# Attention scores of two heads issued alternately on the two halves of TensorE's rows, in a four-layer fp32 decoder trunk

## The chip, the cores and the metric

One core of one Trainium2 chip. The metric is the device time of one execution in microseconds (us), lower is better; times of several runs are given as their median. TensorE (PE) multiplies, VectorE (DVE), ScalarE (ACT) and GpSimd (POOL) work on tiles, SyncE (SP) issues the transfers.

## The reference

Four layers on 256 tokens of width 1024. Each layer has a token mixer with 16 heads of 64 and then a dense SwiGLU feed-forward; after each of the two, `x = LN(alpha * x + f(x))`. The mixers are, in order: sliding-window attention with four key/value heads and a sink logit per head (A), a mixture of three dilated windows merged by their softmax denominators (B), block-sparse attention that at this length is plain causal attention (C), and A again.

```python
    s = jnp.einsum('bnqhgd,bnkhd->bnhgqk', qb, kb) * (dh ** -0.5)
...
    s = jnp.where(ok[None, :, None, None], s, NEG)
    m = s.max(-1)
    if sink is not None:
...
        m = jnp.maximum(m, sk)
    p = jnp.exp(s - m[..., None])
    l = p.sum(-1)
    if sink is not None:
        l = l + jnp.exp(sk - m)
    o = jnp.einsum('bnhgqk,bnkhd->bnqhgd', p, vb) / jnp.transpose(l, (0, 1, 4, 2, 3))[..., None]
```

This is the attention that all three mixers use, over blocks of queries and keys. The dot product of a score runs over the 64 numbers of one head.

## The kernel before, in words

Every fp32 operand of a matrix product is held as two fp16 parts, high and low. A product is three fp16 matmuls into one PSUM bank: high by high, high by low, low by high (`mm3`, lines 127 to 132). Weights come in chunks of 128 x 4096; ACT and DVE make the two parts (`load_w`, lines 91 and 92).

A layer is a projection of the tokens into queries, keys and values (`proj`), attention (`attend`), the output projection (`out_steps`), a layer norm, and the feed-forward (`ffn`). Attention never runs alone: `weave` issues the steps of `attend` evenly between steps of other products. In the mixers' middle part these are the projections of the next heads; at the end (`finish`) they are the output projection. One such fill step is three matmuls of 128 x 512. PE, DVE, ACT and POOL each take their instructions strictly from a list; which instruction stands where in the list is decided when the program is built, from the order in which the steps are issued and from what each waits for, so that pieces of several steps can stand mixed.

Queries and keys lie transposed: tile `qkh` (high part) and `qkl` (low part) hold four pairs of heads, 128 rows by 256 tokens each; rows 0 to 63 are the pair's first head, rows 64 to 127 its second. `halves` picks one head's 64 rows.

`attend` works on items (lines 212 to 305). In A and C an item is two heads of one query tile t of 128 tokens, in B one head with its three groups. Each item goes through four steps, and between them lie whole items: `scores` at once, `flip` two items later (LF), `values` three (LV), `collect` four (LO).

- `scores`: for each head, and each group, one `mm3` of 64 rows into a PSUM bank of 512 columns (pool `ats`, four banks, tile name `at`). With t = 0 it is 128 columns wide, with t = 1 256. DVE then scales, masks and takes the running minimum of the negated scores (line 252), ACT makes the exponentials and their sum (line 255). For A, POOL copies the sinks of the item's two heads beside the scores (line 235).
- `flip`: PE transposes the exponentials in blocks of 128 x 128, up to four blocks in one `at` bank (line 268); ACT and DVE split the bank into parts `ph` and `pl` (lines 135 and 137).
- `values`: `mm3` of `ph`, `pl` with the values into `pv`, 64 columns each; after four heads DVE normalises (line 289).
- `collect`: two transposes of the four heads' result and the split into `oth`, `otl`, the output projection's operand (line 299).

`mixer_a` and `mixer_bc` build the items; the tiles `s` of the scores have four buffers.

Of the kernel before, what the change touches and what calls it, by code (L numbers as in the profile page):

```python
# [18 lines left out]
P = 128  # L19
# [13 lines left out]
# Weights are scaled by a power of two before they are split into two fp16  # L33
# parts, so that the low part stays in fp16's normal range.
# [9 lines left out]
def trunk(ctx, tc, a, out):  # L44
# [99 lines left out]
    def weave(main, fill):  # L144
        """issue two lists of steps, evenly interleaved"""
        nf = 0
        for i, step in enumerate(main):
            step()
            while nf < len(fill) and nf * len(main) < (i + 1) * len(fill):
                fill[nf]()  # L150
                nf += 1
        for step in fill[nf:]:
            step()

    def transpose_x(t, XT, half):
        """columns of X[t] (512 of them) -> XT, in two parts"""
# [32 lines left out]
    def rope(y, t, nh):  # L189
        """y [128, nh, 64] fp32, in place"""  # L190
# [11 lines left out]
    def transpose_qk(y, t, dst):  # L202
        """y [128 tokens, 4 pairs of heads x 128] -> dst parts [128, 4, 256 tokens]"""
# [8 lines left out]
    def attend(items, oT):  # L212
        """steps for softmax attention. items: (query tile, heads, keys of their transposes), with heads [(head, groups, sinks)]
        and groups [(qT, kT, v)]: qT, kT parts [64, 256], v parts [128, NT, 64]; sinks [128, heads]
        (negated) or None. The groups' keys share one softmax. Four heads in a row, of one query tile,
        make a quad, whose outputs are normalised and transposed together."""
        st, quads = {}, {}

        def quad(i):
            t, heads = items[i][:2]  # L220
            return quads.setdefault((t, heads[0][0] // 4), {})

        def scores(i):
            t, heads = items[i][:2]
            flush([(k, tt) for k in items[i][2] for tt in range(t + 1)])
            nk, ng, nh = (t + 1) * P, len(heads[0][1]), len(heads)
            per, n = 512 // nk, nk * ng
            sk, mk = heads[0][2], MASK[heads[0][3]][t]
            q = quad(i)
            if "l" not in q:  # L230
                q["l"] = sm.tile([P, 4], F32, name="l", bufs=6)
            s = sm.tile([P, 768], F32, name="s", bufs=4)
            s = s[:, :nh * (n + (sk is not None))].rearrange("p (h n) -> p h n", h=nh)
            if sk is not None:
                nc.gpsimd.tensor_copy(s[:, :, n], sk)
            mn = sm.tile([P, 4], F32, name="mn", bufs=6)
            ps = None
            for hi, (h, groups, _, _) in enumerate(heads):
                m = None
                for g, (qT, kT, _) in enumerate(groups):  # L240
                    u = hi * ng + g
                    if u % per == 0:
                        ps = ats.tile([P, 512], F32, name="at")
                    o = u % per * nk
                    mm3(ps[:, o:o + nk], sl2(qT, ALL, tok(t)), sl2(kT, ALL, slice(0, nk)), True, True)
                    if u % per == per - 1 or g == ng - 1:
                        # the groups of this head in this bank
                        g0 = max(0, g - u % per)
                        c0, c1 = g0 * nk, (g + 1) * nk
                        init = (3e38 if sk is None else sk[:, hi:hi + 1]) if m is None else m  # L250
                        m = mn[:, 2 * hi + (g0 > 0):2 * hi + (g0 > 0) + 1]
                        nc.vector.tensor_tensor_reduce(  # L252
                            s[:, hi, c0:c1], ps[:, o + nk - (c1 - c0):o + nk], mk[:, c0:c1], scale=-QSC,
                            scalar=init, op0=OP.add, op1=OP.min, accum_out=m)
                nc.scalar.activation(s[:, hi], s[:, hi], AF.Exp, bias=m, scale=-1.0,  # L255
                                     accum_out=q["l"][:, h % 4:h % 4 + 1])
            st[i] = s

        def flip(i):
            t, heads = items[i][:2]  # L260
            nq = len(heads[0][1]) * (t + 1)
            nb = len(heads) * nq
            s, parts = st[i], []
            for b0 in range(0, nb, 4):
                bn = min(4, nb - b0)
                ps = ats.tile([P, 4, P], F32, name="at")
                for b in range(bn):
                    nc.tensor.transpose(ps[:, b], s[:, (b0 + b) // nq, tok((b0 + b) % nq)], ident)
# [3 lines left out]
                parts += [(ph[:, b], pl[:, b]) for b in range(bn)]  # L272
            st[i] = parts

        def values(i):
            t, heads = items[i][:2]
            q, parts = quad(i), st.pop(i)
            if "o" not in q:
                q["o"] = pv[:, turn[0]]
                turn[0] = 1 - turn[0]  # L280
            for h, groups, _, _ in heads:
                nb = len(groups) * (t + 1)
                for b in range(nb):
                    g, kt = divmod(b, t + 1)
                    mm3(q["o"][:, h % 4], parts.pop(0), sl2(groups[g][2], ALL, kt), b == 0, b == nb - 1)
            if h % 4 == 3:
                nc.vector.reciprocal(q["l"], q["l"])
                q["y"] = sm.tile([P, 4, DH], F32, name="oy", bufs=2)
                nc.vector.tensor_tensor(q["y"], q["o"], q["l"].unsqueeze(2).to_broadcast([P, 4, DH]), op=OP.mult)

        def collect(i):
            t, heads = items[i][:2]
            h, q = heads[-1][0], quad(i)
            if h % 4 != 3:
                return
            ps = ats.tile([P, 2, P], F32, name="at")
            y = q["y"].rearrange("p h d -> p (h d)")
            for j in range(2):
                nc.tensor.transpose(ps[:, j], y[:, tok(j)], ident)  # L299
            pr = slice(h // 4 * 2, h // 4 * 2 + 2)  # L300
            split(oT[0][:, pr, tok(t)], oT[1][:, pr, tok(t)], ps)
# [8 lines left out]
    def halves(tq, pr, hh):  # L310
        return sl2(tq, slice(hh * DH, (hh + 1) * DH), pr)
# [3 lines left out]
    def layer_norm(idx, folded=False):  # L315
        """(begin, one(t)): X[t] <- LN(alpha * X[t] + PS[.., t]), and its transposed parts"""
# [38 lines left out]
    def out_steps(PS, lhs, nk, w, h, t, ks, k0=0):  # L355
        """steps of PS[h, t] += lhs.T @ w over the k-tiles ks (of w's, w starting at k0)"""
# [67 lines left out]
    def finish(li, oT, items, kA, folded=False):  # L424
        """the last heads' attention, beside the output projection of the others, and LN"""
# [16 lines left out]
    def mixer_a(li, j, XT):  # L442
# [28 lines left out]
        def items(c):  # L471
            out = []
            for t in range(NT):
                for pr in range(4):
                    heads = []
                    for hh in range(2):
                        h = 8 * c + 2 * pr + hh
                        g = h // 4
                        heads.append((h, [(halves(qTs[c], pr, hh), halves(kT, g, hh), sl2(vv, ALL, ALL, g))],
                                      nsink[:, h - hh:h - hh + 2], 0))  # L480
                    out.append((t, heads, (c, 2)))
# [23 lines left out]
    def mixer_bc(li, XT, ng):  # L505
        """MoBA with one block per sequence has no past block to choose (its selection is masked
        for every query by the shapes alone), which leaves causal attention within the block;
        the dilated groups' softmax merge is one softmax over the groups' keys."""
# [48 lines left out]
        def items(quad):  # L557
            out = []
            for t in range(NT):
                for pr in range(2):  # L560
                    heads = []
                    for hh in range(2):
                        gl = []
                        for g in range(ng):
                            v, off = vs[g, quad]
                            qk = qks[g, quad]
# [153 lines left out]
```

## Time and profile before

| | |
|---|---|
| time, median of 3 runs | 1289.83 us (1288.73 to 1291.22) |
| span of the profiled execution | 1288.2 us (no other time of it is given; the median lies 1.6 us above) |
| PE busy | 1265.8 us, 98% of the span |
| DVE, ACT, POOL busy | 873.0, 664.0 and 112.7 us: 68%, 52%, 9% |
| matmuls | 10352, of them 576 of 64 rows (the scores) |
| granted TensorE clock, mean | 0.997 of full speed |
| DMA | 233 MB, 181 GB/s mean |

A row of the timeline says when an instruction, or several alike, began and how long they took to the last one's end; matmuls are pipelined, so what one costs is read from the start of one to the start of the next. A row of groups has the number of instructions, their busy time and the mean of one, and behind the bar the idle time of the engine just before them and what ended it. A row of stretches has the busy time of each engine in that stretch.

### The profile page before, as it was taken

To read this page: it belongs to the slowest core of one execution; us is meant where nothing else is said; L and a number is where in the kernel's file an instruction comes from. 1 tells how busy PE (TensorE), PEld (TensorE's weight loads), DVE (VectorE), ACT (ScalarE), POOL (GpSimd) and SP (SyncE) were. 2 spreads that over 40 slices of the span, in tenths; PEclk is the share of its full clock that TensorE was granted. 3 is DMA by queue.
4 is the path that set the end of the run, shared out by engine and by line. 5 is a ranking of instruction groups with operands and counts; after the bars stand their busy time and mean duration, and the time that the engine had idled before them with its cause. 6 is when DMAs were issued, how large, how long until landed. Compare 5 with 4: busy or idle time off the path is not lost. (4 is left out here: it accounts for less than half of the span.)

```text
span 1288.2 us, 24678 instructions
## 1 busy us (share of the span) xinstructions
PE 1265.8 (98%) x10352; PEld 844.9 (66%) x10352; DVE 873.0 (68%) x1451; ACT 664.0 (52%) x1117; POOL 112.7 (9%) x230
## 2 busy tenths in 40 slices
PE   7989999999999999999999999999999999999997
PEld 3549988444555555589884445589884445898843
DVE  5888766475565666777665667777665687876652
ACT  5765654345555565446544456536544366464430
POOL 1410000012011101000000020100000041000000
PEclk9999999999999999999999999999999999999999
DMA  8445755656345334347555564247555552475520
GB/s 316 166 164 197 263 200 184 221 206 222 145 147 173 139 131 151 112 163 251 209 181 180 201 225 162 100 164 257 203 180 182 223 207 99 153 250 207 190 87 33
DMA packets 35663, 233.31 MB, mean 181 GB/s; under 512 B 4448, under 2 KB 4448, under 8 KB 9696
## 3 DMA queue, kind: packets, MB, share of 16 engines
q1 hardware_dynamic: 35552, 231.74, 51.0%
q8 instruction: 81, 1.33, 0.4%
q14 instruction: 30, 0.25, 0.1%
HBM read 230.68 MB, written 1.05 MB: 180 GB/s over the span
## 5 line engine op out<-in xcount | busy, mean ns | idle before, releaser
L92 DVE SCALAR_TENSOR_TENSOR wlo<-raw,whi 128x1024 f16<-128x1024 f32 x416 | 500.3, 1223 | 206.1 <-ACT whi L91 205.8
L91 ACT ACTIVATE whi<-raw 128x1024 f16<-128x1024 f32 x416 | 414.6, 1049 | 258.9 <-PE acc L132 92.1
L131 PE MATMUL acc<-xtl,whi 128*128 128x256 f16 (+1 forms) x1792 | 408.2, 250 | 0.0
L132 PE MATMUL acc<-xth,wlo 128*128 128x256 f16 (+1 forms) x1792 | 408.2, 250 | 0.0
L130 PE MATMUL acc<-xth,whi 128*128 128x256 f16 (+1 forms) x1792 | 408.0, 250 | 0.1
L130 PE MATMUL acc<-whi,xth 128*128 128x512 f16 x480 | 183.3, 382 | 2.4 <-ACT xth L135 2.4
L131 PEld LDWEIGHTS <-whi 128*128 128x128 f16 x1792 | 175.3, 98 | 12.5 <-issue 0.3
L130 PEld LDWEIGHTS <-whi 128*128 128x128 f16 x1792 | 175.3, 98 | 11.9
L131 PE MATMUL acc<-wlo,xth 128*128 128x512 f16 x480 | 183.0, 381 | 0.2 <-DVE wlo L92 0.2
L132 PE MATMUL acc<-whi,xtl 128*128 128x512 f16 x480 | 182.8, 381 | 0.3
L132 PEld LDWEIGHTS <-wlo 128*128 128x128 f16 x1792 | 175.3, 98 | 11.6
L130 PE MATMUL acc<-whi,hth 128*128 128x512 f16 x352 | 133.4, 379 | 0.0
L131 PE MATMUL acc<-wlo,hth 128*128 128x512 f16 x352 | 133.4, 379 | 0.0
L132 PE MATMUL acc<-whi,htl 128*128 128x512 f16 x352 | 133.4, 379 | 0.0
L255 ACT ACTIVATE s<-s,mn 128x257 f32<-128x257 f32 (+5 forms) x128 | 67.6, 529 | 46.3 <-DVE mn L252 46.1
L333 POOL TENSOR_TENSOR mv<-mv,nhalf 128x1 f32<-128x1 f32 x16 | 15.8, 986 | 817.5 <-DVE mv L332 817.5
L132 PEld LDWEIGHTS <-xtl 128*128 128x128 f16 x480 | 47.3, 99 | 57.8 <-DVE xtl L137 3.0
L130 PEld LDWEIGHTS <-xth 128*128 128x128 f16 x480 | 47.2, 98 | 48.4 <-issue 5.0
L135 ACT ACTIVATE hth<-hf 128x256 f16<-128x256 f32 x88 | 36.5, 415 | 74.5 <-DVE hf L377 74.5
L131 PEld LDWEIGHTS <-xth 128*128 128x128 f16 x480 | 47.2, 98 | 40.3 <-issue 1.5
L137 DVE TENSOR_TENSOR pl<-at,ph 128x512 f16<-128x512 f32 (+2 forms) x96 | 51.5, 551 | 19.0 <-ACT ph L135 18.5
L132 PEld LDWEIGHTS <-htl 128*128 128x128 f16 x352 | 34.4, 98 | 41.5
(93 smaller groups left out, 1499.0 us busy)
## 6 DMA issues: line engine op xcount, KB each, us to landing
raw<-in_w_gu SPq DMA_DIRECT2D x88, 1024.0 KB, 4.9
raw<-in_w_dn SPq DMA_DIRECT2D x40, 1024.0 KB, 4.9
raw<-in_w_b SPq DMA_DIRECT2D x36, 1024.0 KB, 5.0
raw<-in_w_c SPq DMA_DIRECT2D x12, 1024.0 KB, 4.9
raw<-in_w_a SPq DMA_DIRECT2D x10, 1024.0 KB, 5.5
raw<-in_w_ao SPq DMA_DIRECT2D x8, 1024.0 KB, 6.0
gb<-in_ln_g SPq DMA_DIRECT2D x8, 512.0 KB, 4.6
gb<-in_ln_b SPq DMA_DIRECT2D x8, 512.0 KB, 5.9
```

What stands on the lines that cost most here:

```text
L91: nc.scalar.activation(hi[:, c + d:c + e], r[:, d:e], AF.Copy, scale=WS)
L92: nc.vector.scalar_tensor_tensor(lo[:, c + d:c + e], r[:, d:e], WS, hi[:, c + d:c + e], op0=OP.mult, op1=OP.subtract)
L130: nc.tensor.matmul(ps, st[0], mv[0], start=start, stop=False)
L131: nc.tensor.matmul(ps, st[0], mv[1], start=False, stop=False)
L132: nc.tensor.matmul(ps, st[1], mv[0], start=False, stop=stop)
L135: nc.scalar.activation(hi, src, AF.Copy, scale=1.0 if scale is None else scale)
L137: nc.vector.tensor_tensor(lo, src, hi, op=OP.subtract)
L255: nc.scalar.activation(s[:, hi], s[:, hi], AF.Exp, bias=m, scale=-1.0, accum_out=q["l"][:, h % 4:h % 4 + 1])
L333: nc.gpsimd.tensor_tensor(mv[:, 3:4], mv[:, 2:3], nhalf, op=OP.pow)
```

## The change

An item is now two pairs of heads in A and C (four heads, as many as share a normalisation), and one pair in B. `scores`, `flip`, `values` and `collect` each return a list of small steps, of one or two PSUM banks each, so that fill steps come between them. A score step takes two `at` banks at once, one for each head of a pair. For each of the three part products it issues the first head's matmul on rows 0 to 63 and then the second head's on rows 64 to 127. The lags in items become 1, 2 and 3, and `flip` is issued last in a round instead of second. The `s` tile of an item becomes two, one for the first heads and one for the second ones; each sink is copied alone, so there are 64 copies of one column where there were 32 of two. `flip` fills its banks across all heads of the item: 76 banks in all instead of 96. The number of matmuls, and of DVE's and ACT's instructions on scores, stays.

```diff
-    LAG, LF, LV, LO = 8, 2, 3, 4
+    LAG, LF, LV, LO = 8, 1, 2, 3
...
         def scores(i):
...
-            for hi, (h, groups, _, _) in enumerate(heads):
...
-                    mm3(ps[:, o:o + nk], sl2(qT, ALL, tok(t)), sl2(kT, ALL, slice(0, nk)), True, True)
...
+            def bank_pair(u0):
+                if u0 == 0:
+                    begin()
+                s, q, mn = st[i], quad(i), e["mn"]
+                bank = units[u0:u0 + per]
+                ps = [ats.tile([P, 512], F32, name="at") for _ in range(2)]
+                for b, (pi, g) in enumerate(bank):
+                    qT, kT, _ = pairs[pi][1][g]
+                    for x, y in ((0, 0), (0, 1), (1, 0)):
+                        for hh in range(2):
+                            r = slice(hh * DH, (hh + 1) * DH)
+                            nc.tensor.matmul(ps[hh][:, b * nk:(b + 1) * nk], qT[x][r, tok(t)], kT[y][r, 0:nk],
+                                             start=(x, y) == (0, 0), stop=x == 1)
...
+            return [lambda u0=u0: bank_pair(u0) for u0 in range(0, len(units), per)]
...
-            for fn, lag in ((scores, 0), (flip, LF), (values, LV), (collect, LO)):
+            for fn, lag in ((scores, 0), (values, LV), (collect, LO), (flip, LF)):
                 if 0 <= i - lag < len(items):
-                    steps.append(lambda fn=fn, j=i - lag: fn(j))
+                    steps += fn(i - lag)
```

How PE's list changes is seen at two places. The first is layer B, the second four heads at their first item with t = 1; `acc` is the fill, `at` a score bank, `qkh0` and `qkl0` the parts of group 0. Before:

```order
L132 MATMUL acc_4624<-whi_4610,xtl_3170 128x512
L130 LDWEIGHTS qkh0_3737
L130 MATMUL at_4634<-qkh0_3737 128x256
L131 LDWEIGHTS qkh0_3737
L131 MATMUL at_4634<-qkl0_3738,qkh0_3737 128x256
L132 LDWEIGHTS qkl0_3738
L132 MATMUL at_4634<-qkh0_3737,qkl0_3738 128x256
L130 LDWEIGHTS qkh1_3739
L130 MATMUL at_4634<-qkh1_3739 128x256
```

With the change, at the same place:

```order
L132 MATMUL acc_4526<-whi_4443,xtl_3158 128x512
L256 LDWEIGHTS qkh0_3725
L256 MATMUL at_4559<-qkh0_3725 128x256
L256 LDWEIGHTS qkh0_3725
L256 MATMUL at_4560<-qkh0_3725 128x256
L256 LDWEIGHTS qkh0_3725
L256 MATMUL at_4559<-qkl0_3726,qkh0_3725 128x256
L256 LDWEIGHTS qkh0_3725
L256 MATMUL at_4560<-qkl0_3726,qkh0_3725 128x256
L256 LDWEIGHTS qkl0_3726
L256 MATMUL at_4559<-qkh0_3725,qkl0_3726 128x256
```

Where three matmuls of one head stood in a row on one half, matmuls of two heads now alternate, `at_4559` on the first half and `at_4560` on the second.

The second place is the first layer, the second half of the first eight heads with t = 1 (`xth` is the fill). With the change PE's list has there:

```order
L256 LDWEIGHTS qkl0_183
L256 MATMUL at_538<-qkh1_178,qkl0_183 128x256
L130 LDWEIGHTS xth_99
L130 MATMUL acc_603<-whi_366,xth_99 128x512
L131 LDWEIGHTS xth_99
L131 MATMUL acc_603<-wlo_367,xth_99 128x512
L256 LDWEIGHTS qkh0_182
L256 MATMUL at_539<-qkh1_178,qkh0_182 128x256
```

Here the two heads have come apart: all six matmuls of `at_538` stand ahead of two fill matmuls, all six of `at_539` behind them.

In all of PE's list, the 576 score matmuls stand in 111 unbroken groups before, 104 of them on one half alone, and in 53 with the change, 47 of them on both halves.

## Rows read from the trace of the kernel before

**Rows 1.** The page: the span, and each engine's busy time and instructions.

```profile
span 1288.2 us, 24678 instructions
PE 1265.8 (98%) x10352; PEld 844.9 (66%) x10352; DVE 873.0 (68%) x1451; ACT 664.0 (52%) x1117; POOL 112.7 (9%) x230
```

**Rows 2.** Stretches with attention: length, busy PE, PEld, DVE, ACT, POOL, clock, DMA.

```profile
39.00:100.00 61.00, 57.42 (x451) 32.33 (x450) 54.10 (x139) 41.72 (x108) 11.53 (x24) 0.97 0.42 150
333.00:371.00 38.00, 38.00 (x260) 20.77 (x259) 24.89 (x44) 23.66 (x40) 6.01 (x16) 1.00 0.36 124
...
767.00:840.00 73.00, 72.85 (x528) 38.70 (x526) 53.43 (x136) 46.21 (x116) 9.73 (x25) 1.00 0.35 120
1047.00:1095.00 48.00, 47.60 (x392) 26.27 (x391) 39.78 (x116) 33.52 (x98) 11.57 (x24) 1.00 0.38 132
```

**Rows 3.** Timeline of PE in layer B: nine 128-wide score matmuls on one half.

```profile
334.62 0.38 PE L130 MATMUL acc<-whi,xth 128*128 128x512 f16 x1
...
335.05 0.38 PE L132 MATMUL acc<-whi,xtl 128*128 128x512 f16 x1
335.36 0.23 PE L130 MATMUL at<-qkh 64*128 64x128 f16 x1
335.43 0.22 PE L131 MATMUL at<-qkl,qkh 64*128 64x128 f16 x1
...
335.82 0.22 PE L132 MATMUL at<-qkh,qkl 64*128 64x128 f16 x1
335.97 0.39 PE L130 MATMUL acc<-whi,xth 128*128 128x512 f16 x1
```

**Rows 4.** Timeline of PE, first layer: six 256-wide on two halves, then three on one.

```profile
82.27 0.38 PE L132 MATMUL acc<-whi,otl 128*128 128x512 f16 x1
82.58 0.29 PE L130 MATMUL at<-qkh,qkh 64*128 64x256 f16 x2
...
83.02 0.39 PE L130 MATMUL acc<-whi,oth 128*128 128x512 f16 x1
...
85.52 0.38 PE L132 MATMUL acc<-whi,otl 128*128 128x512 f16 x1
85.83 0.28 PE L130 MATMUL at<-qkh,qkh 64*128 64x256 f16 x1
...
86.26 0.39 PE L130 MATMUL acc<-whi,oth 128*128 128x512 f16 x1
```

**Rows 5.** Groups of the whole span: one third of each width of score matmuls.

```profile
L131 PE MATMUL at<-qkl,qkh 64*128 64x256 f16 x96 | 25.3, 270 | 0.0
L131 PE MATMUL at<-qkl,qkh 64*128 64x128 f16 x96 | 18.1, 216 | 0.0
```

**Rows 6.** Groups on DVE: its score instructions in 39 to 100 us.

```profile
L252 DVE CUSTOM_DVE_ANT_0 s<-at,masks,nsink 128x256 f32<-128x256 f32 x16 | 7.4, 481 | 1.8 <-PE at L132 1.8
L252 DVE CUSTOM_DVE_ANT_0 s<-at,masks,nsink 128x128 f32<-128x128 f32 x16 | 5.1, 350 | 2.0 <-PE at L132 1.9
```

**Rows 7.** The same in 1047 to 1095 us.

```profile
L252 DVE CUSTOM_DVE_ANT_0 s<-at,masks,nsink 128x256 f32<-128x256 f32 x16 | 7.5, 481 | 4.2 <-PE at L132 4.2
L252 DVE CUSTOM_DVE_ANT_0 s<-at,masks,nsink 128x128 f32<-128x128 f32 x16 | 4.9, 347 | 0.7 <-PE at L132 0.6
```

**Rows 8.** The same in 767 to 840 us.

```profile
L252 DVE CUSTOM_DVE_ANT_0 s<-at,masks 128x256 f32<-128x256 f32 x16 | 6.8, 422 | 2.7 <-PE at L132 2.7
...
L252 DVE CUSTOM_DVE_ANT_0 s<-at,masks 128x128 f32<-128x128 f32 x16 | 4.3, 286 | 5.3 <-PE at L132 5.2
```

**Rows 9.** Waits of PE in 1040 to 1098 us: total, times, longest.

```profile
PE at L130 <- DVE mn L252: 0.4, 1, 0.4
```

**Rows 10.** Groups of the whole span: DVE's splits of `flip`, and the sink copies.

```profile
L137 DVE TENSOR_TENSOR pl<-at,ph 128x512 f16<-128x512 f32 x40 | 27.4, 684 | 10.7 <-ACT ph L135 10.5
...
L137 DVE TENSOR_TENSOR pl<-at,ph 128x256 f16<-128x256 f32 x40 | 16.5, 418 | 1.3 <-ACT ph L135 1.0
...
L235 POOL COPY s<-nsink 128x2 f32<-128x2 f32 x32 | 12.0, 391 | 66.2 <-PE at L268 45.4 <-DVE nsink L446 14.7 <-PE pv L132 4.1
```

More of the change, by code (lines that the diff above doesn't have):

```diff
@@ L219, in quad @@
         def quad(i):
-            t, heads = items[i][:2]
-            return quads.setdefault((t, heads[0][0] // 4), {})
+            t, pairs = items[i][:2]
+            return quads.setdefault((t, pairs[0][0] // 2), {})
         def scores(i):
-            t, heads = items[i][:2]
-            flush([(k, tt) for k in items[i][2] for tt in range(t + 1)])
-            nk, ng, nh = (t + 1) * P, len(heads[0][1]), len(heads)
+            t, pairs, keys = items[i]
+            nk, ng = (t + 1) * P, len(pairs[0][1])
@@ L227, in scores @@
             per, n = 512 // nk, nk * ng
[L228 to L236, printed above, removed]
@@ L257, in scores, with begin @@
-            st[i] = s
-        def flip(i):
[L260 to L264, printed above, removed]
+            sk, mk = pairs[0][2], MASK[pairs[0][3]][t]
+            units = [(pi, g) for pi in range(len(pairs)) for g in range(ng)]
+            m, e = {}, {}
+            def begin():
+                flush([(k, tt) for k in keys for tt in range(t + 1)])
+                q = quad(i)
+                if "l" not in q:
+                    q["l"] = sm.tile([P, 4], F32, name="l", bufs=6)
+                st[i] = [sm.tile([P, 768], F32, name="s", bufs=4)[:, :len(pairs) * (n + (sk is not None))].rearrange(
+                    "p (h n) -> p h n", h=len(pairs)) for _ in range(2)]
+                if sk is not None:
+                    for pi, pair in enumerate(pairs):
+                        for hh in range(2):
+                            nc.gpsimd.tensor_copy(st[i][hh][:, pi, n:n + 1], pair[2][:, hh:hh + 1])
+                e["mn"] = sm.tile([P, 8], F32, name="mn", bufs=6)
@@ L265, in flip, with bank @@
+            return [lambda u0=u0: bank_pair(u0) for u0 in range(0, len(units), per)]
+        def flip(i):
+            t, pairs = items[i][:2]
+            n = len(pairs[0][1]) * (t + 1)
+            nb = 2 * len(pairs) * n
+            def bank(b0):
                 bn = min(4, nb - b0)
@@ L267, in flip @@
                 for b in range(bn):
-                    nc.tensor.transpose(ps[:, b], s[:, (b0 + b) // nq, tok((b0 + b) % nq)], ident)
+                    h, c = divmod(b0 + b, n)
+                    nc.tensor.transpose(ps[:, b], st[i][h % 2][:, h // 2, tok(c)], ident)
                 ph = sm.tile([P, 4, P], F16, name="ph")
@@ L271, in flip @@
                 split(ph[:, :bn], pl[:, :bn], ps[:, :bn])
-                parts += [(ph[:, b], pl[:, b]) for b in range(bn)]
-            st[i] = parts
+                parts.setdefault(i, []).extend((ph[:, b], pl[:, b]) for b in range(bn))
+            return [lambda b0=b0: bank(b0) for b0 in range(0, nb, 4)]
+        parts = {}
         def values(i):
[L276 to L289, printed above, removed]
@@ L291, in collect @@
-        def collect(i):
[L292 to L301, printed above, removed]
+            t, pairs = items[i][:2]
@@ new lines, in one @@
+            def one(pr, groups):
+                q = quad(i)
+                if "o" not in q:
+                    q["o"] = pv[:, turn[0]]
+                    turn[0] = 1 - turn[0]
+                for hh in range(2):
+                    nb = len(groups) * (t + 1)
+                    for b in range(nb):
+                        g, kt = divmod(b, t + 1)
+                        mm3(q["o"][:, (2 * pr + hh) % 4], parts[i].pop(0), sl2(groups[g][2][hh], ALL, kt), b == 0,
+                            b == nb - 1)
+                if pr % 2 == 1:
+                    nc.vector.reciprocal(q["l"], q["l"])
+                    q["y"] = sm.tile([P, 4, DH], F32, name="oy", bufs=2)
+                    nc.vector.tensor_tensor(q["y"], q["o"], q["l"].unsqueeze(2).to_broadcast([P, 4, DH]), op=OP.mult)
@@ new lines, in values, with go @@
+            return [lambda p=p: one(p[0], p[1]) for p in pairs]
+        def collect(i):
+            t, pairs = items[i][:2]
+            pr = pairs[-1][0]
+            if pr % 2 == 0:
+                return []
+            def go():
+                ps = ats.tile([P, 2, P], F32, name="at")
+                y = quad(i)["y"].rearrange("p h d -> p (h d)")
+                for j in range(2):
+                    nc.tensor.transpose(ps[:, j], y[:, tok(j)], ident)
+                split(oT[0][:, pr - 1:pr + 1, tok(t)], oT[1][:, pr - 1:pr + 1, tok(t)], ps)
+            return [go]
@@ L473, in items @@
             for t in range(NT):
[L474 to L481, printed above, removed]
+                for q in range(2):
+                    pairs = []
+                    for pr in (2 * q, 2 * q + 1):
+                        g = 2 * c + q
+                        v = sl2(vv, ALL, ALL, g)
+                        h = 8 * c + 2 * pr
+                        pairs.append((h // 2, [(sl2(qTs[c], ALL, pr), sl2(kT, ALL, g), (v, v))],
+                                      nsink[:, h:h + 2], 0))
+                    out.append((t, pairs, (c, 2)))
             return out
@@ L559, in items @@
             for t in range(NT):
+                pairs = []
                 for pr in range(2):
[L561 to L566, printed above, removed]
-                            gl.append((halves(qk, pr, hh), halves(qk, 2 + pr, hh),
-                                       sl2(v, ALL, ALL, off + 2 * pr + hh)))
-                        heads.append((4 * quad + 2 * pr + hh, gl, None, 1 if ng == 1 else 2))
-                    for hs in ([heads] if ng == 1 else [heads[:1], heads[1:]]):
-                        out.append((t, hs, [(g, quad) for g in range(ng)]))
+                    gl = []
+                    for g in range(ng):
+                        v, off = vs[g, quad]
+                        qk = qks[g, quad]
+                        gl.append((sl2(qk, ALL, pr), sl2(qk, ALL, 2 + pr),
+                                   [sl2(v, ALL, ALL, off + 2 * pr + hh) for hh in range(2)]))
+                    pairs.append((2 * quad + pr, gl, None, 1 if ng == 1 else 2))
+                keys = [(g, quad) for g in range(ng)]
+                out += [(t, ps, keys) for ps in ([pairs] if ng == 1 else [pairs[:1], pairs[1:]])]
             return out
```

33 lines of the change are left out of this document (15 added, 18 removed).

## The prediction

> **What bounds the kernel now.** I read the page's totals first [rows 1]: PE is busy 1265.8 of 1288.2 us, DVE 873.0, ACT 664.0. A busy PE need not be a full one, so the next question is whether it ever waits. The stretches with attention [rows 2] answer by layer. In the first layer (A, 39 to 100 us) PE is busy 57.42 of 61 us and DVE 54.10; in a stretch of B, which stands for its four, PE is busy all 38 us and DVE 24.89; in C PE 72.85 of 73 with DVE 53.43; in the last A PE 47.60 of 48 with DVE 39.78. So in B and C PE's own list is the time: what leaves it leaves the span. In the two A layers DVE is nearly as full, and a saving on PE may meet it.
>
> What a score matmul costs is read from starts. In B, nine 128-wide ones on one half [rows 3] stand between two 512-wide fill matmuls that start at 335.05 and 335.97: 0.92 us. A 512-wide matmul among its like takes 0.215 (the fill of 334.62 and the one two further, at 335.05), which leaves 0.70. Inside, 0.39 us from 335.43 to 335.82 are seven steps of 0.056. Nine of them are 0.50; the other **0.20 us is a fixed price of every unbroken group of 64-row matmuls**, partly ahead of it (0.31 from the fill's start to the first score) and partly behind (0.15 from the last score to the next fill). Three 256-wide ones alone, the second part of [rows 4], take 0.74 - 0.215 - 0.20 = 0.325, so 0.109 each with what the rounding leaves.
>
> The decisive rows are the first part of [rows 4]. Between the fills at 82.27 and 83.02 lie six 256-wide matmuls, two at each start ("x2"), three of each head of a pair. They take 0.75 - 0.215 - 0.20 = 0.33 us: the time of three. The two halves already run side by side in this kernel when both heads stand in one group. But only 7 of the 111 groups in PE's list hold both heads.
>
> **The change, part by part.** All on PE first, price 0.20 per group, 0.056 and 0.109 per matmul; the numbers of groups are counted in PE's list, that of matmuls is in [rows 5] (three times 96 of each width).
>
> - Before: 111 x 0.20 + 288 x (0.056 + 0.109) = 22.2 + 47.5 = 69.7 us. By layer: A 26 groups, 48 matmuls of each width: 5.2 + 7.9 = 13.1. B four times 8 groups, 36 of each: 1.6 + 5.9 = 7.5. C 28 groups: 5.6 + 7.9 = 13.5. Last A 25 groups: 5.0 + 7.9 = 12.9.
> - After, where the heads alternate, half of the columns go: A 9 groups, 1.8, and 4.0 for the halves; but twelve 256-wide ones have come apart into two groups of one head each (the second place of PE's list), which adds 0.65, and offsets of some 0.1: 6.6. B 6 groups: 1.2 + 3.0 = 4.2. C 9: 1.8 + 4.0 = 5.8. Last A 11, with twelve of each width come apart: 2.2 + 4.0 + 1.0 = 7.2.
> - Gain on PE: A 6.5, B 4 x 3.3 = 13.2, C 7.6, last A 5.7; together **33.0 us**.
>
> B and C take their gain in full. In B nothing else is near its limit: with 3.3 us less in 38, DVE's 24.89 are 72%. In C, DVE stood idle 2.7 + 5.3 = 8.0 us just before its score instructions because the scores were late [rows 8]; that is what earlier scores give back, and it covers 7.6. In A, the same idle time is 1.8 + 2.0 = 3.8 us [rows 6], in the last A 4.2 + 0.7 = 4.9 [rows 7]. Beyond that DVE, not PE, would have to get shorter. So the first A gives between 3.8 and 6.5, the last between 4.9 and 5.7. I take 4 and 5, near the lower ends, because DVE fills 89% of the first stretch [rows 2] and its row is the nearest.
>
> The edits off this path. `flip` fills 76 banks instead of 96; in an A layer eight splits of 256 columns become four of 512: 8 x 0.418 - 4 x 0.684 = 0.6 us less on DVE [rows 10]. I count it as nothing, since it only softens DVE's bound; with DVE as the end it is worth up to 1.2 us over both layers. The 32 more sink copies cost POOL at most 32 x 0.391 = 12.5 us [rows 10] over two layers, where it is busy 11.5 of 61 and 48 us: covered, unless a late sink holds an exponential. The lags: `values` comes sooner after its `flip`, but the work that stands in PE's list between a bank's last transpose and its first use adds up, at the steps above, to over 0.86 us in all cases but one, before and after alike, so nothing is added. A step that takes two of the four banks at once may wait for DVE to free the second. Bounds: nothing (PE waited once for such a bank in the last A, 0.4 us [rows 9]), and two DVE instructions, 2 x 0.481 = 1.0 us [rows 6], per step; I take nothing, as the row of a wait that occurred is nearest, and because the tightest reuses of a bank have more work ahead of them in PE's list than before.
>
> Sum: 4 + 13.2 + 7.6 + 5 = 29.8 us. The profiled execution's span becomes 1288.2 - 29.8 = 1258.4; the median of the runs lies 1.6 above that span, so **1260.0 us**.
>
> The Trainium skill (TensorEngine Tiling (Array Packing), Performance Considerations, PSUM Bottleneck) speaks against so much: tiling makes TensorE faster but not the emptying of PSUM, which can become the bottleneck. By that rule the layers with a full DVE would give nothing, and the next part prices that; the rows side with it in the first A and against it in B.
>
> **The rivals.**
>
> 1. *DVE becomes the bound wherever it is busy.* For it: 54.10 of 61 us, 39.78 of 48 and 53.43 of 73 [rows 2]; DVE's score work does not change. Against it: 3.8, 4.9 and 8.0 us of idle time that late scores caused [rows 6 to 8], and DVE can postpone weight parts into the feed-forward. If only B gains: 1289.8 - 13.2 = 1276.6.
> 2. *Alternating matmuls do not overlap*, because each has its own weight load between, on the other half. Then only 58 fewer groups remain: 58 x 0.20 = 11.6 us, 1278.2. Against it: in [rows 4] each of the six had its own load too, and the two heads' first matmuls began at one time although the list had them head after head.
> 3. *Slower: PE waits at the two-bank steps.* PE takes its list in order, so one missing bank also holds all fill behind it. An item's four DVE reductions last 4 x 0.48 = 1.9 us [rows 6], and the 24 items of A and C (four heads each), with fewer fill steps than B, might each wait for the set of the step before: 24 x 1.9 = 46 us, against 29.8: 1306. It decides from 33 us of new waits, 1.4 us per item. Against it: such a wait occurs once now [rows 9], and fewer banks are asked for in all.
>
> That the change doesn't do what it says is excluded by PE's list: 47 of the 53 groups hold both heads.
>
> **How the numbers follow.** My forecast 77%, rival 1 10%, rival 2 7%, rival 3 4%, and 2% for waits that eat about all of the gain. The forecast's own range: full gain in A, with A's present waits shrinking by some 2 us, 1289.8 - 35 = 1254.5; and half of what A and C give, 1289.8 - 13.2 - 8.3 = 1268. To hold 8 in 10 it must reach rival 1: 1254 to 1277. A measurement tells about 0.2% (2.6 us) from no change. Faster: the first three cases, 0.94; the same 0.02; slower 0.04.
>
> **What would show it.** Right: in B, between two fills, eighteen 128-wide matmuls in 0.50 + 0.20 us, two at each start, and B's four stretches shorter by about 3.3 us each with PE without waits; C shorter by 7 or more; A by 4 with DVE over 93% busy. Wrong: one start at a time in alternating groups (rival 2); C and the last A not shorter with DVE idle only after ACT (rival 1); PE waits on line 256 named after DVE, above 1 us per item (rival 3), or a granted clock that falls behind such waits as it did in the first A, whose mean is 0.97 [rows 2].

## The result, and the profile after

The change takes 1270.62 us, median of four runs (1270.34 to 1272.11); the kernel before, run beside it, 1289.93 (1288.73 to 1291.22). The ratio is 0.9854 (0.984 to 0.9868): 19.3 us faster, where 29.8 were forecast. The direction was right and the time lies in the range, but a third of the gain is missing.

The page after, to be set beside [rows 1]:

```profile
span 1268.3 us, 24652 instructions
PE 1238.2 (98%) x10352; PEld 829.0 (65%) x10352; DVE 868.7 (68%) x1431; ACT 657.4 (52%) x1097; POOL 126.2 (10%) x262
```

PE is busy 27.6 us less, and the span is 19.9 us shorter. PE did less work, then, and stood still more than before. Stretches that answer those of [rows 2], in the same columns, show where (first A, B, C, last A; those of A and C are shorter now, that of B is another piece of its layer, with 316 matmuls where 260 stood):

```profile
39.00:97.60 58.60, 52.99 (x457) 30.56 (x456) 53.07 (x135) 40.29 (x105) 14.56 (x36) 0.97 0.50 173
330.00:369.00 39.00, 39.00 (x316) 21.61 (x317) 28.18 (x51) 25.90 (x45) 11.18 (x20) 1.00 0.42 142
753.00:822.00 69.00, 66.59 (x525) 36.41 (x524) 51.06 (x131) 44.91 (x112) 11.16 (x29) 1.00 0.36 127
1029.00:1076.00 47.00, 44.80 (x404) 26.17 (x403) 40.37 (x116) 32.66 (x94) 11.46 (x36) 1.00 0.38 135
```

In C, PE stood idle 0.15 of 73 us before and 2.41 of 69 now; in the last A 0.40 of 48 and 2.20 of 47; in the first A 3.58 of 61 and 5.61 of 58.6. In the middle of B it never stops.

**The scores did what was forecast.** The timeline of PE in B, to be set beside [rows 3]:

```profile
329.60 0.38 PE L132 MATMUL acc<-whi,xtl 128*128 128x512 f16 x1
329.91 0.23 PE L256 MATMUL at<-qkh 64*128 64x128 f16 x2
329.98 0.22 PE L256 MATMUL at<-qkl,qkh 64*128 64x128 f16 x2
...
330.37 0.22 PE L256 MATMUL at<-qkh,qkl 64*128 64x128 f16 x2
330.52 0.39 PE L130 MATMUL acc<-whi,xth 128*128 128x512 f16 x1
```

Two start together every 0.056 us. Eighteen matmuls fit between two fills 0.92 us apart, where nine fitted in 0.92 before.

**Where the rest went.** For each matmul of the trace one can take the time from its start to the next one's start, less the usual step of its kind (0.215 for 512 columns, 0.109 for 256 and for fp32 of 128, 0.056 for 128, 0.029 for 64). What is over, from 0.03 us up, is put down to the instruction that came late. For a group of score matmuls everything between the two surrounding steps is counted. Whole kernel, in us:

| | before | after | |
|---|---|---|---|
| score groups: A, B, C, last A | 13.5, 30.1, 13.4, 13.0 | 7.3, 16.7, 6.0, 8.2 | -31.8 |
| late start of `values` | 1.6 | 10.2 | +8.6 |
| late start of `collect`'s transposes | 0.8 | 4.7 | +3.9 |
| late start of other transposes | 8.9 | 10.7 | +1.8 |
| late start of fill | 11.8 | 9.6 | -2.2 |

The sum is -19.7. The fill's row holds the stretches at a lower clock too, of which the first A has one in either kernel. By phase, from the first projection matmul of a layer to its first feed-forward matmul (the feed-forwards stayed at 174.7 to 175.0 us each):

| | first A | B | C | last A |
|---|---|---|---|---|
| before | 92.0 | 280.8 | 114.5 | 84.4 |
| after | 88.6 | 270.6 | 110.6 | 82.3 |
| difference | -3.4 | -10.2 | -3.9 | -2.1 |
| forecast | -4 | -13.2 | -7.6 | -5 |

The view of PE's waits over the whole span names the new ones (total, times, longest; it counts from a matmul's modelled end, 0.38 us after its start, and so finds less than a count by starts):

```profile
PE at L324 <- DVE oy L311: 3.4, 2, 2.5
PE pv L130 <- ACT ph L135: 3.0, 7, 0.7
PE pv L132 <- DVE pl L137: 2.6, 7, 0.8
...
PE at L256 <- DVE qkl L137: 0.8, 1, 0.8
PE at L285 <- ACT s L271: 0.8, 3, 0.4
...
PE at L256 <- DVE otl L137: 0.2, 1, 0.2
```

Before, the same view had these four among its rows, and none for `ph`:

```profile
PE acc L132 <- DVE otl L137: 1.8, 2, 1.4
PE pv L130 <- DVE oy L289: 0.5, 1, 0.5
PE pv L132 <- DVE pl L137: 0.5, 2, 0.3
PE at L268 <- ACT s L255: 0.4, 1, 0.4
```

One such wait in C, from the timelines of all three engines after:

```profile
758.40 0.60 PE L285 MATMUL at<-ident,s 128*128 128x128 f32 x4
...
759.24 0.50 ACT L271 ACTIVATE s<-s,mn 128x256 f32<-128x256 f32 x1
759.24 2.33 DVE L92 SCALAR_TENSOR_TENSOR wlo<-raw,whi 128x1024 f16<-128x1024 f32 x2
760.13 0.60 PE L206 MATMUL at<-ident,qkv 128*128 128x128 f32 x4
...
760.71 0.50 ACT L271 ACTIVATE s<-s,mn 128x256 f32<-128x256 f32 x1
761.00 0.38 PE L132 MATMUL acc<-whi,xtl 128*128 128x512 f16 x1
761.21 0.58 ACT L135 ACTIVATE ph<-at 128x512 f16<-128x512 f32 x1
761.82 0.69 DVE L137 TENSOR_TENSOR pl<-at,ph 128x512 f16<-128x512 f32 x1 [0.24 <-ACT ph L135]
761.84 0.20 PE L130 MATMUL pv<-hth,ph 128*128 128x64 f16 x1 [0.46 <-ACT ph L135]
...
762.56 0.20 PE L132 MATMUL pv<-hth,pl 128*128 128x64 f16 x1 [0.49 <-DVE pl L137]
```

PE transposed the bank in four steps from 758.40 on, to 758.84, and its list then held 2.4 us of other work, to 761.22. ACT comes to the split of the bank only at 761.21, behind four exponentials that it began at 759.24; DVE can begin only when `ph` is there, and takes 0.69 us for a full bank. PE, whose list has `values` next, does nothing else meanwhile: between 761.00 and 762.69 it issues one fill matmul and six of 64 columns. The banks are fuller than before [rows 10]:

```profile
L137 DVE TENSOR_TENSOR pl<-at,ph 128x512 f16<-128x512 f32 x68 | 45.6, 683 | 13.5 <-ACT ph L135 13.3
...
L137 DVE TENSOR_TENSOR pl<-at,ph 128x256 f16<-128x256 f32 x8 | 3.3, 416 | 2.6 <-ACT ph L135 2.6
```

Before, 40 of the 96 splits were 256 wide and 40 were 512 wide; now 68 of 76 are 512 wide. On ACT they take 0.590 us here; before, 256 columns took 0.379. The way from bank to `values` is 0.590 + 0.683 = 1.27 us where it was 0.379 + 0.418 = 0.80 for those: 0.47 us more, beside the 2 us of exponentials that stood ahead of the split here.

The longest wait is at the end of the first A. PE and DVE there:

```profile
88.94 1.41 DVE L358 SCALAR_TENSOR_TENSOR x<-x,mv,gb 128x512 f32<-128x512 f32 x2
89.13 0.38 PE L131 MATMUL acc<-wlo,oth 128*128 128x512 f16 x1
90.26 1.41 DVE L360 SCALAR_TENSOR_TENSOR x<-x,mv,gb 128x512 f32<-128x512 f32 x2
91.58 0.42 DVE L311 TENSOR_TENSOR oy<-pv,l 128x256 f32<-128x256 f32 x1
92.06 0.69 PE L324 MATMUL at<-ident,oy 128*128 128x128 f32 x2 [2.55 <-DVE oy L311]
```

The division `oy`, 0.42 us, stands on DVE behind the layer norm of the other query tile. Towards the end of this wait, at 91.7 us, the granted clock falls to the lower level, 1.2 GHz: it is 0.97 in the 4 us with the wait and 0.51 in the stretch behind it (length, PE, PEld, DVE, ACT, POOL, clock, DMA):

```profile
88.00:92.00 4.00, 1.51 (x14) 0.54 (x10) 4.00 (x8) 0.04 (x1) 0.99 (x1) 0.97 0.00 0
92.00:95.20 3.20, 3.14 (x10) 1.70 (x11) 1.88 (x5) 0.38 (x1) 0.00 (x0) 0.51 0.28 41
```

The row of the waits on line 256 that names `qkl` is a wait for a score bank. In the last A:

```profile
1029.19 0.60 PE L206 MATMUL at<-ident,qkv 128*128 128x128 f32 x4
...
1029.72 0.23 PE L256 MATMUL at<-qkh,qkh 64*128 64x128 f16 x2
...
1030.91 0.23 PE L256 MATMUL at<-qkh,qkh 64*128 64x128 f16 x1
...
1031.84 0.68 DVE L137 TENSOR_TENSOR qkl<-at,qkh 128x512 f16<-128x512 f32 x1
...
1032.43 0.34 DVE L266 CUSTOM_DVE_ANT_0 s<-at,masks,nsink 128x128 f32<-128x128 f32 x1
1032.57 0.21 PE L256 MATMUL at<-qkh,qkh 64*128 64x128 f16 x1 [0.83 <-DVE qkl L137]
```

At 1030.91 the first heads of a step take one bank, and their six matmuls read the same tiles that the second heads' matmul at 1032.57 reads, so that one does not wait for its operands. All four `at` banks are taken: two by the scores of 1029.72, which DVE first reads at 1032.43, one by those of 1030.91, one by the transposes of 1029.19. DVE's pass `qkl` reads the last of these and ends at 1032.52. By starts PE is 0.9 us late here, and 0.4 us at 65 us, where it waits for DVE's pass `otl` over another such bank.

### The profile page after: what moved, and what is told of

It reads as the page before. It is cut to its first block, busy times and chain, and to the rows that moved or that the text cites. A ratio compares the mean times of both kernels' runs of the same rounds, so it can differ in the third digit from the quotient of the medians.

```text
span 1268.3 us, 24652 instructions
## 1 busy us (share of the span) xinstructions
PE 1238.2 (98%) x10352; PEld 829.0 (65%) x10352; DVE 868.7 (68%) x1431; ACT 657.4 (52%) x1097; POOL 126.2 (10%) x262
## 3 DMA queue, kind: packets, MB, share of 16 engines
HBM read 230.68 MB, written 1.05 MB: 183 GB/s over the span
## 5 line engine op out<-in xcount | busy, mean ns | idle before, releaser
L91 ACT ACTIVATE whi<-raw 128x1024 f16<-128x1024 f32 x416 | 414.5, 1049 | 260.0 <-PE acc L131 89.1
L131 PEld LDWEIGHTS <-hth 128*128 128x128 f16 x352 | 34.4, 98 | 40.8
```

Of the source, the lines that this page charges most:

```text
L91: nc.scalar.activation(hi[:, c + d:c + e], r[:, d:e], AF.Copy, scale=WS)
```

## The experiments

**Theory 1**: the gain on the scores is whole; what is missing are waits for `ph`, `pl` and `oy`, because `values` and `collect` now stand too few steps behind what they read. **Rival a**: DVE's own work bounds the A layers and C, so that any wait removed comes back elsewhere. **Rival b**: the halves are not independent, and only strict alternation (or only fewer groups) helps.

**e1_flip_first_ac.** In A and C a round issues scores, flip, values, collect. B keeps the changed order: the new one would need more buffers of `ph` and `pl` there.

```diff
-            for fn, lag in ((scores, 0), (values, LV), (collect, LO), (flip, LF)):
+            order = ((scores, 0), (values, LV), (collect, LO), (flip, LF))
+            if len(items[0][1][0][1]) == 1:
+                order = ((scores, 0), (flip, LF), (values, LV), (collect, LO))
+            for fn, lag in order:
```

> The changed kernel, but in A and C a round issues flip right after scores, ahead of values and collect (B as it is: it would need more ph and pl buffers). Theory 1, the missing 10 us are PE's new waits of values and collect for their splits, because flip now stands last in a round and values soon after it: these waits (about 7.5 us in A and C) shrink by half or more, 1265 to 1268 us. Theory 2, DVE is full in A and C and sets their length in whatever order: 1270.6 within 1 us, the waits only move to other instructions.

Measured: 1264.91 us, ratio 0.9811 (0.9798 to 0.9825). The phases are 87.1, 270.6, 107.9 and 81.3. In C the late starts of `values` fall from 2.83 to 0.12 us. In 750 to 822 us PE waits once, 0.2 us, and its row of that stretch is nearly full again:

```profile
750.00:822.00 72.00, 71.49 (x563) 39.92 (x562) 52.62 (x134) 45.23 (x113) 11.13 (x29) 1.00 0.37 131
```

So in C the distance was the cause: the same work, 2.7 us shorter, and a DVE at 73%. In the first A the waits partly move. Those of `values` fall from 3.1 to 1.6 and those of `collect` from 3.0 to 0.5, but there is a new one, and within the layer's phase other transposes start late by 6.2 instead of 2.9 us:

```profile
PE at L160 <- DVE x L363: 1.2, 1, 1.2
```

**e9_values_later.** The changed order, with lags 1, 3, 4 in A and C instead of 1, 2, 3.

```diff
+        more = 1 if len(items[0][1][0][1]) == 1 else 0
...
-            for fn, lag in ((scores, 0), (values, LV), (collect, LO), (flip, LF)):
+            for fn, lag in ((scores, 0), (values, LV + more), (collect, LO + more), (flip, LF)):
```

> The changed kernel with its order in a round, but values and collect one item later in A and C (lags 1, 3, 4; B as it is). Theory 1, the distance from flip to values is what was too short: like flip first, the waits of values in A and C (7.5 us) fall by half or more, 1264 to 1268. If it is the place of flip in the round (its transposes come too late for DVE and ACT), and not the distance: 1269 to 1271.

Measured: 1265.41 us, 0.9818 (0.9805 to 0.9832); phases 86.3, 270.6, 108.6, 81.4. Another edit that lengthens the same distance gives the same time as e1 within the intervals: it is the distance, not the order of the round.

**e2_head_by_head.** In a step, all matmuls of the first head, then all of the second.

```diff
-                for b, (pi, g) in enumerate(bank):
-                    qT, kT, _ = pairs[pi][1][g]
-                    for x, y in ((0, 0), (0, 1), (1, 0)):
-                        for hh in range(2):
+                for hh in range(2):
+                    for b, (pi, g) in enumerate(bank):
+                        qT, kT, _ = pairs[pi][1][g]
+                        for x, y in ((0, 0), (0, 1), (1, 0)):
```

> The changed kernel, but a step issues all matmuls of the first head of a pair and then all of the second; groups and steps are the same. If the two halves take their matmuls independently of each other once both stand in one unbroken group: 1270.6 within 1.5 us, and pairs with one start in the timeline. If matmuls start strictly in the order of the list, so that alternating is what makes them overlap: all but the neighbours of the border run one after another, some 17 us more, 1287 to 1289.

Measured: 1273.75 us, 0.9879 (0.9866 to 0.9893), 3.1 above the change and between the two times expected; phases 88.8, 274.1, 109.9, 82.5. The score groups of B cost 21.0 us instead of 16.7. The timeline of PE in B shows how the second head begins:

```profile
329.96 0.38 PE L132 MATMUL acc<-whi,xtl 128*128 128x512 f16 x1
330.27 0.23 PE L256 MATMUL at<-qkh 64*128 64x128 f16 x1
...
330.56 0.22 PE L256 MATMUL at<-qkh,qkl 64*128 64x128 f16 x1
330.57 0.26 PE L256 MATMUL at<-qkh 64*128 64x128 f16 x2
330.64 0.25 PE L256 MATMUL at<-qkl,qkh 64*128 64x128 f16 x2
...
331.18 0.39 PE L130 MATMUL acc<-whi,xth 128*128 128x512 f16 x1
```

Six of the first head's nine start alone. Then the second head begins beside the last three, which stand ahead of it in PE's list, and 1.22 us lie between the fills instead of 0.92. With six 256-wide matmuls per head it begins 0.24 us after the first, again with three of them to come:

```profile
340.72 0.28 PE L256 MATMUL at<-qkh 64*128 64x256 f16 x1
...
340.96 0.37 PE L256 MATMUL at<-qkh 64*128 64x256 f16 x2
...
341.71 0.39 PE L130 MATMUL acc<-whi,xth 128*128 128x512 f16 x1
```

With three per head, as in [rows 4], it begins at once. The halves do run independently, but in these groups a half starts past at most three waiting matmuls of the other. So rival b holds for long groups: alternation itself is worth 3.1 us here, nearly all of it in B. All score groups together cost 44.9 us instead of 38.3; other late starts, which shrank, give about half of that back.

**e3_heads_apart.** Each head's bank is a step of its own, so that fill stands between the two heads.

```diff
-            def bank_pair(u0):
+            def bank_pair(u0, hh):
...
-                ps = [ats.tile([P, 512], F32, name="at") for _ in range(2)]
+                ps = {hh: ats.tile([P, 512], F32, name="at")}
...
-            return [lambda u0=u0: bank_pair(u0) for u0 in range(0, len(units), per)]
+            return [lambda u0=u0, hh=hh: bank_pair(u0, hh) for u0 in range(0, len(units), per) for hh in range(2)]
```

> The changed kernel, but the bank of the first head and the bank of the second are separate steps with fill steps between where there are any: 84 groups of score matmuls instead of 53, 15 of them on both halves instead of 47. By the prices of the prediction (0.20 us a group, the columns of the longer half) score matmuls cost 57.8 us instead of 36.5. If that price is what the change gained: 1288 to 1293, less what shorter steps save in waits. If the gain came from the smaller steps and the new order instead: near 1270.

Measured: 1284.54 us, 0.9965 (0.9953 to 0.9978), 13.9 above the change; phases 86.0, 284.1, 112.5, 83.1. PE's list has 84 groups, 15 of them on both halves, and the scores cost 61.5 us instead of 38.3: +23.2. It is less slow than that because its waits are fewer: those of `values` 5.2 us instead of 10.2, those of `collect` 1.9 instead of 4.7. So the two heads side by side are the gain of the change, and the new distances are a loss.

**e4_spaced_ends.** Two blank steps behind an attention list's last flip and behind its last values, so that two steps of fill go there.

```diff
                     steps += fn(i - lag)
+                    if i - lag == len(items) - 1 and fn in (flip, values):
+                        steps += [lambda: None] * 2
```

> The changed kernel, but where an attend list runs empty two blank steps stand behind the last flip and two behind the last values, so that the even weaving puts more fill there. Theory 1 with the waits mostly at these ends (B's waits at 432, 447 and 515 to 539 us, the last collects of A at 89 and 1080 us): 3 to 5 us less, 1266 to 1268. If the waits come from the order inside the rounds: 1270 within 1 us; if DVE sets the time: the same 1270.

Measured: 1266.76 us, 0.9824 (0.9811 to 0.9838); phases 85.1, 271.0, 110.6, 81.9. The first A gives 3.5 us: `collect`'s transposes start late by 0.14 us there instead of 2.97, and no stretch at the lower clock follows. B and C give nothing; in C, 12 score groups where there were 9 cost 7.4 us instead of 6.0.

**e5_both, e6_first_and_collect, e7_one_blank.** e1 with the blanks of e4; with blanks behind the last values alone; with one blank instead of two.

> Flip right after scores in A and C, and the blank steps at the ends of the lists, together. Theory 1, both cut the same kind of wait (PE for a split or a normalisation that was issued too short before): they partly add, 1261 to 1264 us, with the waits of values and collect together under 5 us. If they remove the same waits: 1265, as flip first alone. If DVE is full: 1265 or above.

> As the run with both, but blank steps only behind the last values, ahead of the last collect. Theory 1: with flip first in A and C, what is left at the ends is the wait of the last collect (1.2 us in the last A, 0.5 in the first): 1263 to 1264.5 us.

> As the run with both, but one blank step at each of the two places instead of two. Theory 1: between flip first alone and the run with both, 1262 to 1264.5 us; fill that goes to the ends is missing elsewhere, so that fewer blanks can also be the better.

Measured: 1268.95 us, 0.9845 (0.9831 to 0.9858); 1268.06, 0.9838 (0.9825 to 0.9852); 1266.74, 0.9829 (0.9816 to 0.9843). All three missed, and all are slower than e1 alone. The phases of e5 are 87.2, 271.0, 110.2, 81.8. In C the blanks break the alternating groups (12 groups, 7.4 us, as in e4), and in the first A `collect`'s transposes are late by 2.4 us again. e5 also lies where its expectation puts a full DVE, but these rows name other causes. Each edit shifts all steps that follow in the layer, so what two edits give apart does not add within a layer.

**e12_by_layer.** The changed order with blanks in the A layers, flip first in C, B as changed.

```diff
-            for fn, lag in ((scores, 0), (values, LV), (collect, LO), (flip, LF)):
+            order = ((scores, 0), (values, LV), (collect, LO), (flip, LF))
+            if len(items[0][1][0][1]) == 1 and items[0][1][0][2] is None:
+                order = ((scores, 0), (flip, LF), (values, LV), (collect, LO))
+            for fn, lag in order:
                 if 0 <= i - lag < len(items):
                     steps += fn(i - lag)
+                    if i - lag == len(items) - 1 and fn in (flip, values) and items[0][1][0][2] is not None:
+                        steps += [lambda: None] * 2
```

> Each layer as it was shortest so far: A with the changed kernel's order and blank steps at the ends (85.1 and 81.9 us from its first projection to the feed-forward), B as changed (270.6), C with flip first (107.9). If the layers' lengths add, as they did in the runs so far: 1.4 us less than flip first, 1263 to 1264 us. If a layer's list also depends on the others': anything up to 1267.

Measured: 1263.72 us, 0.9801 (0.9788 to 0.9814); phases 84.5, 270.6, 107.9, 81.9. Between layers the lengths do add: the A layers are those of e4 within 0.6 us, C is that of e1. This is the lowest time of a kernel that does all the work, 26 us below the kernel before and 6.9 below the change; its interval overlaps those of e1 and e9.

**e10_less_dve and e11_before_less_dve.** To test rival a, the A layers' output bias and the residual passes that carry it are left out (the output lacks it), once in e1 and once in the kernel before. That takes 3.1 us from DVE in each A layer (two passes of 1.22, one of 0.71) and nothing from PE.

```diff
-        nc.vector.tensor_scalar(bo, bo, WS, None, op0=OP.mult)
-        for t in range(NT):
-            nc.vector.scalar_tensor_tensor(X[t], X[t], ALPHA * WS, bo, op0=OP.mult, op1=OP.add)
-        return finish(li, oT, items(1), 4, True)
+        return finish(li, oT, items(1), 4, False)
```

> Flip first in A and C, with the A layers' output bias left out (its scaling and two residual instructions of 1.22 us on DVE fall away, some 3.5 us of DVE per A layer; the residual's factor goes into the layer norm's own instruction, so nothing is added). If DVE's total sets the length of the A layers now: 4 to 7 us less than flip first, 1258 to 1261. If single chains set it: 1263 to 1265.

> The kernel before, with the same output bias left out. If DVE was not yet the bound of the A layers there, less than the change gives with flip first: 0 to 3 us, 1287 to 1290. If DVE was the bound already: 4 to 7 us less, 1283 to 1286, and the change never had more to gain there than DVE's idle time.

Measured: 1263.65 us, 0.9795 (0.9782 to 0.9809), phases 84.4, 270.6, 107.9, 82.4; and 1285.44, 0.9968 (0.9956 to 0.9981), phases 87.9, 280.8, 114.5, 84.0. By their times e10 falls into the range expected of single chains, e11 into that of a full DVE. The first A loses 2.7 us against e1 and 4.1 against before, where a stretch at the lower clock (77.8 to 81.2 us) went too; at half the clock that stretch held 1.7 us less work, so some 2.4 of the 4.1 are left for DVE (an estimate). The last A is 1.1 us longer than in e1 (a stretch of 3.4 us at the lower clock came up there, behind a wait of 1.5 us for a score bank) and 0.4 shorter than before. So less work on DVE shortens the first A in either order. That DVE's total is a bound there does not follow: e12 reaches 84.5 us in it with all of that work, as short as e10 without it, and e4 takes 3.5 us from the changed kernel's first A and leaves DVE's work as it is. In the last A neither run shows that DVE is the bound.

**e8_pool_residual.** The same residual work moved to POOL, in e1.

```diff
-        nc.vector.tensor_scalar(bo, bo, WS, None, op0=OP.mult)
+        nc.gpsimd.tensor_scalar(bo, bo, WS, None, op0=OP.mult)
         for t in range(NT):
-            nc.vector.scalar_tensor_tensor(X[t], X[t], ALPHA * WS, bo, op0=OP.mult, op1=OP.add)
+            nc.gpsimd.tensor_scalar(X[t], X[t], ALPHA * WS, None, op0=OP.mult)
+            nc.gpsimd.tensor_tensor(X[t], X[t], bo, op=OP.add)
```

> Flip first in A and C, and in the A layers the scaling of the output bias and of the residual (one 128x1024 product, and two of 1.22 us, on DVE before) go to POOL. Theory: with flip first the A layers are bound by DVE, which is busy 57.8 of the 61 us from 39 to 100. Then some 3.5 us less on DVE per A layer give 2 to 5 us in all, 1260 to 1263. If chains of single waits, not DVE's total, set the A layers: 1264.9 within 1 us; slower if the layer norm waits for POOL.

Measured: 1276.95 us, 0.9904 (0.9891 to 0.9918); phases 89.8, 270.6, 107.9, 89.1. The groups of lines and PE's waits of this run tell why:

```profile
L526 POOL TENSOR_TENSOR x<-x,htl 128x1024 f32<-128x1024 f32 x4 | 11.3, 2830 | 0.1
```

```profile
PE at L206 <- ACT qkv L491: 6.1, 2, 5.5
PE at L206 <- POOL qkv L200: 5.1, 1, 5.1
```

The rotary step `qkv` stands behind these adds in POOL's list, and PE waits 5.1 us for it and 6.1 us for `qkv` from ACT. This run put new waits in place of the old work, and so it decides nothing about DVE.

## Why the prediction was right, and where it failed

- **The price of the scores: right.** Summed by layer, 69.5 us were read for before and 36.4 for after, taken as a gain of 33.0; the trace has 70.1 and 38.3, a gain of 31.8. 0.20 us per group, 0.056 and 0.109 per matmul and full overlap of the halves hold; some 1.8 us of the 38.3 are waits inside groups. Rival 2 falls with this row, and e3 shows it from the other side.
- **"The lags: ... nothing is added": this step failed.** It cost 8.6 us before `values` and 3.9 before `collect`'s transposes, 12.5 of the 33 saved. The step compared distances in PE's list with 0.86 us, before and after alike. The case shown in C had 2.4 us there and was still late: `values` began 3.0 us after the bank's last transpose, and its first matmul on `pl` 0.7 us later. The step left out what stands at the other end: four exponentials ahead of the split on ACT, some 2 us, weight parts of 1.2 us each on DVE, and splits of 512 columns where 40 of 96 had been 256 wide (1.27 us instead of 0.80). It also left out the end of a list, where no later item stands between `oy` and its transposes. That the distance was too short is shown by e1 and e9 in C and by e4 at the end of the first A; no run tells apart what the queues and what the wider banks add.
- **"B and C take their gain in full": wrong by that same cost.** C gave 3.9 instead of 7.6; with the distance restored (e1) it gave 6.6, and 1.1 of late transposes were left. B gave 10.2 instead of 13.2. The late starts of `values` in B, 2.7 us where there were none, are about the difference. The runs that moved B's steps, those with blanks at the ends of its lists (e4 to e7), gave nothing there (271.0 in e4, with 2.2 of them left): that the distance is their cause there is argued, not shown.
- **The A layers.** "I take 4 and 5, near the lower ends, because DVE fills 89% of the first stretch": the first A gave 3.4 and DVE is at 91% there (53.07 of 58.6 us), below the 93% that was named as the sign. That the size is near is luck: e4 gets 3.5 us more with DVE's work untouched, so what held the changed kernel there was the wait for `oy` and the clock behind it rather than DVE's total. The Trainium skill (TensorEngine Tiling (Array Packing), Performance Considerations, PSUM Bottleneck) warns that packing does not speed up what empties PSUM: the trace agrees in part for the first A, where less work on DVE helps (e10, e11), and not for the stretch shown of B, where PE never stops and DVE is at 72%. The last A gave 2.1 instead of 5. The score groups gave 4.8 there; the late starts of `values` and `collect` took 2.6 back. e1 and e4 recovered only 0.9 and 0.4 of it: 1.8 and 1.6 us of such late starts remain in their last A, and what holds it stays open.
- **"A step that takes two of the four banks at once ... I take nothing": nearly right.** No row of PE's waits names DVE's score passes, but two name DVE passes over other `at` banks (`qkl`, `otl`), and PE was 1.3 us late there in all. That is most of what the score groups cost above their price. Rival 3, 1.4 us or more per item, did not occur.
- **`flip` and the sinks: right.** DVE's total fell by 4.3 us without effect on B's or C's time; the 64 sink copies cost POOL 17.8 us instead of 12.0, and no exponential's wait names them.
- **Rival 1** (1276.6, only B gains) did not occur: the first A gave 3.4, C 3.9, the last A 2.1, and in C e1 shows the distance as the cause and not DVE.
- **The range.** The forecast's own range, 1254.5 to 1268, misses 1270.62; the stated one holds it only because it was stretched to reach rival 1. (1289.8 - 35 is 1254.8, not 1254.5; this changes nothing.) Of the signs named for "right", eighteen matmuls between two fills with two at each start came; 3.3 us from each stretch of B, 7 or more from C and a DVE over 93% in A did not.

To 1260.0 the best version still lacks 3.7 us, of which the late starts in B hold up to 2.7.

## What to carry to other kernels

When a change fuses or regroups steps, recompute the whole way from producer to consumer at the new tile size and behind the other work of those engines; the same number of list places is not the same cover. Look at the last items of each list apart: in the first A nothing followed them that could hide a wait. And lay out each stage's list for itself: here one order served C, another the A layers, and both edits in one layer undid each other.

## What was not expected of the hardware

- The two row halves of TensorE take matmuls out of the list's order, each half its own, so that PE does not take its list quite strictly: in e2 the second head began while up to three of the first head's matmuls, listed ahead of it, had not started, in groups of nine, of six and of three alike. Farther ahead than that no half was seen to run.
- A single PE wait of 2.55 us was followed by a granted clock of 0.51 for 3.2 us, in which 512-wide fills came 0.43 us apart instead of 0.215. In e4, without that wait, the stretch was gone, and the first A 3.5 us shorter. It needs no single long wait: in the kernel before, PE was busy 1.68 of the 3.8 us up to 77.8, with late starts of up to 1.05 us, and the 3.4 us behind them ran at 0.50.
- POOL took 2.83 us in the mean of four (2.34 to 3.32) for an add of 128x1024 in fp32 (e8), where DVE scales and adds the same tile in 1.21 (e1).
